# w_out's sums, the start of the feed-forward and the pooling of a hybrid encoder block: other places in the order of work

## The chip, the cores and the metric

The kernel runs on one core of a Trainium2 chip. The metric is the device time of one execution in microseconds (us). The core's engines are named as in the profile: PE (TensorE, matmuls), DVE (VectorE), ACT (ScalarE), POOL (GpSimd) and SP (SyncE, whose queue issues all DMAs here). Each engine works through its own queue in order and waits at an instruction until that instruction's inputs, and the room for its output, are there.

## The reference

One layer of a bidirectional encoder trunk on x of 1024 tokens by 1024 channels, float32:

```python
h = rmsnorm(x, norm_mix)
proj = h @ w_in            # q, k, v, r, decay low-rank, pool input u, gates g_a, g_b
o = gla_fwd(q, k, v) + gla_bwd(q, k, v)          # 4 heads
o = per_head_rmsnorm(o) * gla_norm * silu(r)
y_a = o @ w_branch_gla
pooled = window_means(u, (2, 4, 8, 16)) - u       # 4 groups of 128 channels
y_b = (pooled @ w_pool_group, per group) * pool_scale
x = x + (sigmoid(g_a) * y_a + sigmoid(g_b) * y_b) @ w_out
h2 = rmsnorm(x, norm_ffn)
gate, up = split(h2 @ w_ffn_in)                   # 2 x 2816
x = x + (silu(gate) * up) @ w_ffn_out
return rmsnorm(x, norm_final)
```

## The kernel before, in words

**Products.** Every float32 operand is held as a high part (a cast on ACT, `wh`, `dh`, `gh`, `oh`) and a low part (source minus high part on DVE or POOL, `wl`, `dl`, `gl`, `ol`). A product of two operands is three matmuls, high by high, high by low, low by high (`products`, `mm3`). The large matrix products are done by Strassen's scheme in Winograd's form: seven products P1 to P7 of sums of blocks instead of eight of blocks. S1 to S4 are the sums of the left operand's blocks: S1 = a21 + a22, S2 = S1 - a11, S3 = a11 - a21, S4 = a12 - S2. P6 takes S2, P5 takes S1, P7 takes S3 and P3 takes S4.

**The order.** The whole order of instructions is written out by hand: each engine gets its instructions in the order in which the Python code issues them. What runs beside the matmuls is issued by `pump`, which every `mm3` calls with the length of its product (1 for 512 columns). `soon(delay, step)` issues a step after so many products, `settle` issues at once all that was put off, `begin(generator, delay)` starts a side job that yields the number of products to its next step.

**Gate units (`Gates`, ten of them, n = 0 to 9).** Each runs P1 to P7 of four `mm3` each, in the order `run_of` gives. Units 0 and 1 make the pool input u, which is stored to `u_rows`; 2 to 9 make the gates. Weight parts are made four products ahead (`gates_ahead`, AHEAD). POOL also makes the sums of w_out's blocks (`output_jobs`, L599) beside units 0 to 2. `pooling` is a side job: for each of four groups it loads u, then `pooled` makes for each half the window sums on DVE (L995, L1001, L1007, L1009), a cast on ACT (L1013) and a low part on DVE (L1015). Its yields are multiplied by POOLING = 1.75.

**Branch and w_out (`project`).** Both are seven products of two halves each, so 28 pieces: 0 to 13 for the branch, order `BRANCH`, 14 to 27 for w_out, order `MERGED` = P1, P4, P6, P7, P5, P2, P3. In each piece PE does eight `mm3`: four row tiles m, two k. Each piece has three steps in `line`: its load, its `sums` (of blocks), its `make` (cast and low part of the data, cast and low part of the weights). At piece n `project` makes piece n+2, and asks for the sums by `line_sums`:

```python
line_load()
line_make()
line_sums()
```

`line_make` also calls `line_sums` where the sums of the piece it makes were not begun. Since two pieces are made at the end of the gate units, `line_sums()` at piece n begins those of piece n+3. After the second half of a product `collect` adds each row tile's bank onto x (L1507, DVE) or merges the branch (L1351, L1353, L1354). P1, P6 and P7 of w_out accumulate in one set of four banks, one after the other. In w_out `merged` holds the blocks in slots of their own, 39 slots in all; the sums of P6 write S1 and S2 over blocks, S3 goes to a slot of its own (`s3s`), and S4 is written over block (0, 1) as the sums of P3.

**Norm before the feed-forward.** As P5, P2 and P3 of w_out finish rows of x, `collect_out` takes the squares on ACT, and `normed` scales one row tile after the other: `two_scale` adds both halves' means (L1489, DVE) and takes the power -0.5 (L1490, POOL), and `scale_by` scales the tile (L306, DVE). `features(0)` and `features(1)` then transpose it on PE and make the sums, high and low parts that the feed-forward reads (`split_b`).

**Feed-forward.** 22 units, `run` of `Gated`; the first run of units mixes units 0, 1 and 2, and `features(1)` is made beside it. Units 0 and 1 read ready weight parts from DRAM (`ReadyUnit`). The output stage follows, and the final norm, where `two_scale` is used too.

Of the kernel before, what the change touches and what calls it, by code (L numbers as in the profile page):

```python
# [33 lines left out]
FT = D_FF // P  # L34
# [17 lines left out]
def kernel(  # L52
# [937 lines left out]
    def pooled(g, u, hi, lo):  # L990
        width = WINDOWS[g]
        n = HALF + 2 * PAD
        for half in range(2):
            s = t2(n, s="ws")
            nc.vector.tensor_tensor(s[:, 1:n], u[half][:, : n - 1], u[half][:, 1:n], op=ALU.add)  # L995
            yield 1
            lo_p, hi_p, step = 1, n, 1
            while 2 * step < width:
                a = t2(n, s="ws")
                lo_p, hi_p = lo_p + step, hi_p - step  # L1000
                nc.vector.tensor_tensor(  # L1001
                    a[:, lo_p:hi_p], s[:, lo_p - step : hi_p - step], s[:, lo_p + step : hi_p + step], op=ALU.add
                )
# [5 lines left out]
            nc.vector.scalar_tensor_tensor(  # L1009
                s[:, body], s[:, body], 1.0 / width, u[half][:, body], op0=ALU.mult, op1=ALU.subtract  # L1010
            )
            yield 1
            nc.scalar.copy(hi[:, half, :], s[:, body])  # L1013
            yield 1
            nc.vector.tensor_tensor(lo[:, half, :], s[:, body], as_f32(hi[:, half, :]), op=ALU.subtract)  # L1015
            yield 0.2

# [5 lines left out]
        if len(loads) < len(line):  # L1023
            loads.append(line[len(loads)][0]())

    def line_sums():
        if len(begun_sums) < len(line):
            begun_sums.append(line[len(begun_sums)][1]())

    def line_make():  # L1030
# [76 lines left out]
    MERGED = (1, 4, 6, 7, 5, 2, 3)  # L1107
    WEIGHT_B = {1: (0, 0), 2: (1, 0), 3: (1, 1)}
    merged = {}
    s3s = []  # L1110

    def merged_piece(p, c):
        def load():
            if p in WEIGHT_B:
                i, j = WEIGHT_B[p]
                return weight_load(chunk(w_out, i, j, c))
            return weight_load(t_wo[p][:, 2 * c : 2 * c + 2, :])

        def sums():
            def block(i, j):  # L1120
                return merged[i, j][c][:, :, :]

            if p == 6:
                s3s.append(slot(s="s3"))
                sub(s3s[c][:, :, :], block(0, 0), block(1, 0))
                padd(block(1, 0), block(1, 0), block(1, 1))
                sub(block(0, 0), block(1, 0), block(0, 0))
            elif p == 3:
                sub(block(0, 1), block(0, 1), block(0, 0))

        def make(raw):
            a = s3s[c] if p == 7 else merged[{1: (0, 0), 6: (0, 0), 5: (1, 0), 4: (1, 1), 2: (0, 1), 3: (0, 1)}[p]][c]
            return data_split(a), weight_split(raw)

        return load, sums, make
# [117 lines left out]
    for n, run in enumerate(gate_runs):  # L1253
# [10 lines left out]
        for at, (of, p) in enumerate(run):  # L1264
            if not gates_ahead.step() and at in (5, 7):
                line_make()
            zs[of].run(p)
            for _ in range(2 * (at == 0 and not last)):
                gunits[n + 1].load()
            if p in (7, 4):  # L1270
                zs[of].store(int(p == 4))
            if at == 4:
                flush()
                if n == 2:
                    begin(pooling(), 4)
# [22 lines left out]
    def project(base, products, collect, before, amid=None, first=FIRST, up=UP, pools_of=lambda p: U_BANKS if p == 1 else X_BANKS):  # L1298
        banks = {}
        for at, p in enumerate(products):  # L1300
# [4 lines left out]
            for c in range(2):  # L1305
# [4 lines left out]
                    settle()  # L1310
                line_load()
                line_make()
                line_sums()
                if c == 1 and amid:
                    amid(p)
                a, b = made[n]
# [70 lines left out]
    class ReadyUnit(Unit):  # L1387
# [14 lines left out]

    units = [ReadyUnit(n) if n < READY else Unit(w_ffn_in, (f * P, D_FF + f * P)) for n, f in enumerate(f_order)]

    unit_runs = [[(n, p) for p in (1, 2) for n in range(3)] + [(n, p) for p in (5, 6, 3, 7) for n in range(2)]]
    unit_runs.append([(2, 5), (0, 4), (1, 4), (2, 6), (2, 3), (2, 7)])
    unit_runs += [run_of(n, 2) for n in range(3, FT)]
    unit_runs[-1] = last_run(FT - 1)
    units_ahead = Ahead(units, chain(
        unit_runs[0], [(2, 5), (0, 4), (1, 4), (2, 6), (2, 3), (2, 4), (2, 7)], *(steps_of(n, n == FT - 1) for n in range(3, FT))  # L1410
    ))


# [7 lines left out]
    def low_block(p, i, src, eng=nc.vector):  # L1421
        hi, lo = split_b[p][i]
        eng.tensor_tensor(lo[:, :, :], src, as_f32(hi[:, :, :]), op=ALU.subtract)  # L1423
        if i == 1:
            split_done.add(p)

    def features(half):

# [6 lines left out]
        for k in range(KT):  # L1435
# [13 lines left out]
            elif k % 2:  # L1449

                t = block(0, 0, i)
                if k < 4:
                    sub(t, block(0, 1, i), t)
                    cast_block(5, i, t)
                else:
                    low_block(5, i, t)
                    sub(t, block(1, 1, i), t)
                    cast_block(6, i, t)
            yield 2 if half == 0 else 2.5 if k % 2 else 1
        if half == 0:  # L1460
            return

        for i in range(2):
            cast_block(3, i, block(1, 1, i))
            low_block(6, i, block(0, 0, i))
            yield 3
        for p, b in ((7, block(0, 1, 0)), (7, block(0, 1, 1)), (4, block(1, 0, 0)), (4, block(1, 0, 1))):
            i = len(split_b.get(p, ()))
            if p == 7:
# [16 lines left out]

    def two_scale(ms):
        rs = vec(1, "n3rs")
        nc.vector.tensor_scalar(rs[:, :], ms[:, 0:1], ms[:, 1:2], EPS, op0=ALU.add, op1=ALU.add)  # L1489
        nc.gpsimd.tensor_tensor(rs[:, :], rs[:, :], half_neg[:, :1], op=ALU.pow)  # L1490
        return rs

# [4 lines left out]
    def normed(keep=0):  # L1497
        while len(unnormed) > keep:
            t = unnormed.pop(0)
            scale_by(xn[t], x2[t][:, :], two_scale(mss[t]))  # L1500
            flush()
            later(x2_out[t], x2[t][:, :])

# [26 lines left out]
                units_ahead.step()  # L1530

    def amid_out(p):
        if p == 3:
            for _ in range(2):
                units_ahead.step()

# [121 lines left out]
            both.append((hi, lo))  # L1658
        ready_pieces.append(both)

    begin(features(1), 12)
    zs = {n: Gated(units[n], True) for n in range(3)}
    out_sums, summing = [OutSums(0)], None

    early = {1: "l", 2: "l", 3: "s", 4: "l", 5: "s", 6: "ls"}
    done = {}
    for n, run in enumerate(unit_runs, 1):
        if n == 2:
            finish_side()
            zs[2].two_sums()  # L1670
# [160 lines left out]
```

## Time and profile before

| | us |
|---|---|
| median of three runs | 1402.03 (1400.65 to 1402.65) |
| the profiled execution | 1400.65 |
| its span, first to last instruction | 1398.9 |
| PE busy | 1368.4 (98%) |
| DVE, POOL, ACT busy | 849.5, 748.3, 625.6 |
| granted TensorE clock | 0.999 |

A row of a group names line, engine, operation, output<-inputs and shapes, then the count, the busy time and the mean of one. A row of the timeline begins with start and length in us from the span's start; brackets at its end hold the idle time of the engine before it and what ended it. A row of the waits says who waited for whom, the total in us, how many times, and the longest. In the profile PE is called busy while matmuls overlap, so that idle time of PE is found by the waits and by the start of one matmul after the other.

### The profile page before, as it was taken

What the parts mean: (1) busy time and instruction counts of PE and PEld (TensorE: products, weight loads), DVE (VectorE), ACT (ScalarE), POOL (GpSimd) and SP (SyncE); (2) the same over time, 40 slices, a digit from 0 to 9 for tenths busy, and PEclk for the clock granted to TensorE, in tenths of its full rate; (3) what the DMA queues carried; (4) which work ended last, traced back from release to release, by engine and by line L of the source; (5) the groups of instructions that cost most, each with busy time, mean ns of one, the idle gap of its engine ahead of it and who ended that gap; (6) DMA issues with size and microseconds to landing.
All of it is one profiled execution on the core that took longest, in us unless ns stands there. A gap on an engine that the chain in (4) does not pass through costs nothing.

```text
span 1398.9 us, 18565 instructions
## 1 busy us (share of the span) xinstructions
PE 1368.4 (98%) x6677; PEld 1152.5 (82%) x6677; DVE 849.5 (61%) x1073; ACT 625.6 (45%) x1117; POOL 748.3 (53%) x558
## 2 busy tenths in 40 slices
PE   7999999999999999999999999999999999999997
PEld 6889898978888878788887788888888888888876
DVE  6256757567745975687875865556565556343363
ACT  6364655564233444455346633333333334453253
POOL 3242626031378456568665176666666667454354
PEclk9999999999999999999999999999999999999999
DMA  6212404341268667996515455554444447975461
GB/s 193 76 45 61 136 37 137 102 125 53 76 199 281 213 209 232 354 404 244 200 71 180 166 181 174 173 173 159 145 141 149 140 154 254 388 255 218 165 234 67
DMA packets 167612, 243.62 MB, mean 174 GB/s; under 512 B 10936, under 2 KB 98016, under 8 KB 167520
## 3 DMA queue, kind: packets, MB, share of 16 engines
q1 hardware_dynamic: 167520, 242.45, 51.3%
q8 instruction: 52, 0.85, 0.2%
q14 instruction: 40, 0.33, 0.1%
HBM read 164.55 MB, written 77.86 MB: 173 GB/s over the span
## 4 chain that ended last, share of the span: by engine, by line
PE 81%; DVE 7%; ACT 3%; issue 3%; POOL 3%; DMA 2%; SPq 0%; POOLq 0%; DVEq 0%; ACTq 0%
PE ps L270 74%; PE op L797 2%; POOL wl L197 1%; PE kv L270 1%; PE sc L733 1%; PE op L270 1%; PE tr L317 1%; DMA u_out<-uph 1%; DVE z L666 1%; PE ps L448 1%; DVE fs L866 0%; DMA gor<-g_out 0%; DMA wor<-t_out 0%; DVE so L725 0%; ACT wh L196 0%
## 5 line engine op out<-in xcount | busy, mean ns | idle before, releaser
L197 POOL TENSOR_TENSOR wl<-fs,wh 128x512 fp32r<-128x512 f32 x120 | 166.1, 1388 | 164.8 <-ACT wh L196 139.5
L270 PE MATMUL ps<-gl,wh 128*128 128x512 f32 x616 | 239.8, 389 | 0.9 <-DVE gl L1423 0.9
L270 PE MATMUL ps<-gh,wh 128*128 128x512 f32 x616 | 240.4, 390 | 0.0
L270 PE MATMUL ps<-gh,wl 128*128 128x512 f32 x616 | 239.7, 389 | 0.0
L197 POOL TENSOR_TENSOR wl<-fraw,wh 128x512 fp32r<-128x512 f32 x90 | 129.2, 1436 | 58.2 <-ACT wh L196 57.8
L197 POOL TENSOR_TENSOR ol<-gor,oh 128x1024 fp32r<-128x1024 f32 (+1 forms) x42 | 100.3, 2394 | 93.1 <-ACT oh L196 84.7
L270 PE MATMUL ps<-hh,wh 128*128 128x512 f32 x376 | 149.8, 398 | 0.0
L270 PE MATMUL ps<-hh,wl 128*128 128x512 f32 x376 | 146.7, 390 | 0.0
L270 PE MATMUL ps<-hl,wh 128*128 128x512 f32 x376 | 146.5, 390 | 0.0
L197 POOL TENSOR_TENSOR wl<-raw,wh 128x512 fp32r<-128x512 f32 x47 | 66.3, 1423 | 147.6 <-ACT wh L196 139.2
L270 PEld LDWEIGHTS ps<-gl,wh 128*128 128x128 f32 x616 | 115.7, 188 | 24.9 <-DVE gl L1423 1.3
L270 PEld LDWEIGHTS ps<-gh,wl 128*128 128x128 f32 x616 | 115.7, 188 | 24.2
L270 PEld LDWEIGHTS ps<-gh,wh 128*128 128x128 f32 x616 | 115.7, 188 | 23.6
L270 PE MATMUL ps<-oh,oh 128*128 128x512 f32 x308 | 119.9, 389 | 1.2 <-DVE x L1753 1.2
L270 PE MATMUL ps<-ol,oh 128*128 128x512 f32 x308 | 120.0, 389 | 0.2 <-DVE ol L197 0.2
L270 PE MATMUL ps<-oh,ol 128*128 128x512 f32 x308 | 119.8, 389 | 0.0
L197 POOL TENSOR_TENSOR wl<-wraw,wh 128x512 fp32r<-128x512 f32 x56 | 89.9, 1633 | 45.0 <-ACT wh L196 44.9
L197 DVE TENSOR_TENSOR ol<-wor,oh 128x1024 fp32r<-128x1024 f32 (+1 forms) x42 | 62.0, 1496 | 54.4 <-ACT oh L196 47.1
L196 ACT CAST wh<-fs 128x512 fp32r<-128x512 f32 x120 | 73.8, 615 | 28.8 <-DVE fs L866 28.7
L270 PEld LDWEIGHTS ps<-hh,wl 128*128 128x128 f32 x376 | 70.6, 188 | 15.0
L270 PEld LDWEIGHTS ps<-hl,wh 128*128 128x128 f32 x376 | 70.7, 188 | 13.4
L270 PEld LDWEIGHTS ps<-hh,wh 128*128 128x128 f32 x376 | 70.7, 188 | 13.3
(249 smaller groups left out, 3183.1 us busy)
## 6 DMA issues: line engine op xcount, KB each, us to landing
fraw<-in_w_ffn_in_dram SPq DMA_DIRECT2D x44, 512.0 KB, 5.8
gor<-g_out SPq DMA_DIRECT2D x35, 512.0 KB, 6.7
raw<-in_w_in_dram SPq DMA_DIRECT2D x48, 256.0 KB, 3.0
g_out<-s SPq DMA_DIRECT2D x44, 256.0 KB, 2.3
fraw<-in_w_in_dram SPq DMA_DIRECT2D x20, 512.0 KB, 6.7
wor<-t_out SPq DMA_DIRECT2D x20, 512.0 KB
g_out<-g SPq DMA_DIRECT2D x33, 256.0 KB, 2.6
x<-in_x_dram SPq DMA_DIRECT2D x16, 512.0 KB, 5.1
```

What stands on the lines that cost most here:

```text
L196: nc.scalar.copy(hi, src)
L197: eng.tensor_tensor(lo, src, as_f32(hi), op=ALU.subtract)
L270: nc.tensor.matmul(ps, a[i], b[j], start=first and n == 0, stop=last and n == 2, skip_group_check=onto)
L317: nc.tensor.transpose(ps[:, c], xt[:, k * P : (k + 1) * P], ident[:, :])
L448: nc.tensor.matmul(ps[:, :], lw[k // 4][:, k % 4, :, :].rearrange("p a r -> p (a r)"), hT(k, half)[i], start=k == 0 and i == 0, stop=k == ...
L666: nc.vector.tensor_tensor_scan(cs[:, :], cy, la[:, :], 0.0, op0=ALU.mult, op1=ALU.add)
L733: nc.tensor.matmul(sc[d][:, i * CH : (i + 1) * CH], chunk_of(ke, n, d), chunk_of(qe, n, d), start=True, stop=True,)
L797: nc.tensor.matmul(op[:, :DV], a, b, start=False, stop=j == len(terms) - 1)
```

## The change

- Pooling begins in gate unit 1 instead of 2; in `pooled` the yield between the last sum and the cast is 2 instead of 1, and that between cast and low part 1.5 instead of 1.
- `line_sums` takes the number of the piece up to which sums are begun. `project` calls it with n + 2; after P1 of w_out it is called with piece 18, the first half of P6.
- S4 gets slots of its own and is made as the sums of P7; P3 reads it there.
- `two_scale`'s add is on POOL, and `normed` puts `scale_by` off by 1.5 products.
- The feed-forward's first run is P1, P2, P5 of units 0 to 2 and then P6, P3, P7 of units 0 and 1; the second run begins with P4 of both. `features(1)` begins after 11 products instead of 12, and its casts and low parts are put off by 1.5 and 3.3 products (`split_soon`).

```diff
@@ pooled
-            yield 1
+            yield 2
             nc.scalar.copy(hi[:, half, :], s[:, body])
-            yield 1
+            yield 1.5
@@
-    def line_sums():
-        if len(begun_sums) < len(line):
+    def line_sums(to=None):
+        to = len(begun_sums) if to is None else to
+        while len(begun_sums) < min(len(line), to + 1):
             begun_sums.append(line[len(begun_sums)][1]())
@@ merged_piece
-            elif p == 3:
-                sub(block(0, 1), block(0, 1), block(0, 0))
+            elif p == 7:
+                s4s.append(slot(s="s4"))
+                sub(s4s[c][:, :, :], block(0, 1), block(0, 0))
...
+            a = s3s[c] if p == 7 else s4s[c] if p == 3 else merged[
+                {1: (0, 0), 6: (0, 0), 5: (1, 0), 4: (1, 1), 2: (0, 1)}[p]
+            ][c]
@@ gate units
-                if n == 2:
+                if n == 1:
                     begin(pooling(), 4)
@@ project
-                line_sums()
+                line_sums(n + 2)
@@ order of the feed-forward
-    unit_runs = [[(n, p) for p in (1, 2) for n in range(3)] + [(n, p) for p in (5, 6, 3, 7) for n in range(2)]]
-    unit_runs.append([(2, 5), (0, 4), (1, 4), (2, 6), (2, 3), (2, 7)])
+    unit_runs = [[(n, p) for p in (1, 2, 5) for n in range(3)] + [(n, p) for p in (6, 3, 7) for n in range(2)]]
+    unit_runs.append([(0, 4), (1, 4), (2, 6), (2, 3), (2, 7)])
...
+    def split_soon(p, i, src):
+        soon(1.5, partial(cast_block, p, i, src))
+        soon(3.3, partial(low_block, p, i, src))
@@ features(1)
                 if k < 4:
                     sub(t, block(0, 1, i), t)
-                    cast_block(5, i, t)
+                    split_soon(5, i, t)
                 else:
-                    low_block(5, i, t)
+                    settle()
                     sub(t, block(1, 1, i), t)
-                    cast_block(6, i, t)
+                    split_soon(6, i, t)
...
             cast_block(3, i, block(1, 1, i))
-            low_block(6, i, block(0, 0, i))
             yield 3
+            settle()
@@ two_scale, normed
-        nc.vector.tensor_scalar(rs[:, :], ms[:, 0:1], ms[:, 1:2], EPS, op0=ALU.add, op1=ALU.add)
+        nc.gpsimd.tensor_scalar(rs[:, :], ms[:, 0:1], ms[:, 1:2], EPS, op0=ALU.add, op1=ALU.add)
...
-            scale_by(xn[t], x2[t][:, :], two_scale(mss[t]))
+            soon(1.5, partial(scale_by, xn[t], x2[t][:, :], two_scale(mss[t])))
@@ amid_out
-        if p == 3:
+        if p == 1:
+            line_sums(len(BRANCH) * 2 + 4)
+        elif p == 3:
@@ start of the feed-forward
-    begin(features(1), 12)
+    begin(features(1), 11)
     zs = {n: Gated(units[n], True) for n in range(3)}
+    zs[2].two_sums()
...
-            while n == 1 and p > 2 and p not in split_done:
-                next(side[0][0])
+                if put_off:
+                    settle()
+                else:
+                    next(side[0][0])
...
-            if n > 1 and 0 < at + (n == 2) < 6:
+            if n > 1 and 0 < at + 2 * (n == 2) < 6:
                 next(summing, None)
```

More of the change, by code (lines that the diff above doesn't have):

```diff
@@ L1109 @@
     merged = {}
-    s3s = []
+    s3s, s4s = [], []
     def merged_piece(p, c):
@@ L1127, in sums @@
                 sub(block(0, 0), block(1, 0), block(0, 0))
-            elif p == 3:
-                sub(block(0, 1), block(0, 1), block(0, 0))
+            elif p == 7:
+                s4s.append(slot(s="s4"))
+                sub(s4s[c][:, :, :], block(0, 1), block(0, 0))
         def make(raw):
-            a = s3s[c] if p == 7 else merged[{1: (0, 0), 6: (0, 0), 5: (1, 0), 4: (1, 1), 2: (0, 1), 3: (0, 1)}[p]][c]
+            a = s3s[c] if p == 7 else s4s[c] if p == 3 else merged[
+                {1: (0, 0), 6: (0, 0), 5: (1, 0), 4: (1, 1), 2: (0, 1)}[p]
+            ][c]
             return data_split(a), weight_split(raw)
@@ L1409 @@
     units_ahead = Ahead(units, chain(
-        unit_runs[0], [(2, 5), (0, 4), (1, 4), (2, 6), (2, 3), (2, 4), (2, 7)], *(steps_of(n, n == FT - 1) for n in range(3, FT))
+        unit_runs[0], [(0, 4), (1, 4), (2, 6), (2, 3), (2, 4), (2, 7)], *(steps_of(n, n == FT - 1) for n in range(3, FT))
     ))
@@ L1669 @@
             finish_side()
-            zs[2].two_sums()
         elif n > 2:
```

## The prediction

> **What bounds the kernel now.** I read the page's first part, then the waits of PE, then the stretches by engine.
>
> ```profile
> span 1398.9 us, 18565 instructions
> PE 1368.4 (98%) x6677; PEld 1152.5 (82%) x6677; DVE 849.5 (61%) x1073; ACT 625.6 (45%) x1117; POOL 748.3 (53%) x558
> ```
>
> PE is the bound, and the change adds and removes no matmul. So only time in which PE stands can move. The waits of PE between 500 and 790 us:
>
> ```profile
> PE tr L1438 <- DVE xn L306: 1.6, 1, 1.6
> PE ps L270 <- ACT ga L1212: 1.4, 1, 1.4
> PE ps L270 <- DVE x L1507: 1.2, 1, 1.2
> PE yb L270 <- DMA pl<-p_out: 0.9, 1, 0.9
> PE ps L270 <- DVE gl L1423: 0.9, 1, 0.9
> PE ps L270 <- DVE dl L162: 0.7, 1, 0.7
> ```
>
> These six single waits lie where the change works. The rhythm of PE in a stretch without waits, from the chain in order of time:
>
> ```profile
> 367.55 5.48 PE ps L270 x24
> 373.03 0.44 PE tp L970 x4
> ```
>
> A matmul of 512 columns takes 5.48 / 24 = 0.228 us from start to start, so a product (three matmuls) takes 0.68, a piece of `project` (eight products) 5.46, a product of a unit (four) 2.73. A single matmul lasts 0.39 (row below), so a wait costs its idle time and the lost overlap, 0.39 - 0.228 = 0.16. Without the DMA wait, five waits make 5.8 + 5 x 0.16 = **6.6 us**: the most that the change can give. The DMA wait (p_out loads of the last gate units, 56 us after pooling's last sum) stays: these are loads of pooled rows that lie stored long before, and no edit touches what SP holds ahead of them.
>
> **Pooling, 1.6 us.** The stretches, and ACT where PE waited for it:
>
> ```profile
> 424.00:446.00 22.00, 22.00 (x99) 18.23 (x98) 8.32 (x9) 8.55 (x15) 19.16 (x15) 1.00 0.88 286
> 446.00:507.00 61.00, 61.00 (x271) 50.53 (x270) 55.15 (x62) 26.83 (x49) 33.03 (x32) 1.00 0.69 221
> 511.23 0.62 ACT L1013 CAST ph<-ws 128x512 fp32r<-128x512 f32 x1 [2.50 <-DVE ws L1009]
> 511.76 0.58 ACT L1212 COPY ga<-ps 128x512 f32<-128x512 f32 x1
> ```
>
> The columns of the first two are stretch, length, PE, PEld, DVE, ACT, POOL, clock, DMA share, GB/s. While pooling runs, DVE is busy 55.15 of 61. It falls behind, ACT's cast L1013 waits for it, and the copy L1212, which frees a bank, is queued behind the cast. The new yields hold the cast back 3.5 products instead of 1.75 (2.4 us for 1.2) and the low part 2.6 for 1.75. The same DVE work of a half of the last group is spread over 13.5 products instead of 10.85. The cast waited 2.50; a hold longer by 1.2 and 1.8 us more in which DVE can catch up cover that. I count the whole wait as gone, 1.4 + 0.16.
>
> One unit sooner, the first group meets POOL's subtractions (POOL busy 19.16 of 22). Six DVE sums there slow POOL: a 512-wide sum beside DVE takes up to the double of the 1.3 us that it takes alone (rows of w_out below for both engines), so 0 to 8 us in sum, some 3 if half of each overlaps. The weight parts behind it are made four products of a unit (10.9 us) ahead; that hides it. SP is moved past too: the loads of u follow the stores of the same rows directly and hold the queue for a store's landing. The unit's weight loads behind them have the same 10.9 us. Cost nothing; without that cover up to 3 us.
>
> **w_out: sums one piece later, S4 at P7.** In the kernel before, piece n begins the sums of piece n+3, one piece (5.46 us) before that data is cast. In the changed one `line_sums(n + 2)` finds nothing to do, because `line_make` has just forced these sums; only piece 18 (P6, first half) keeps its place, by `amid_out`. So the sums of pieces 12, 13 and 19 come one piece later, straight ahead of the cast of the same data.
>
> ```profile
> 654.00:673.00 19.00, 19.00 (x86) 15.73 (x85) 18.69 (x20) 8.57 (x12) 16.02 (x11) 1.00 0.68 250
> 642.73 2.32 DVE L1084 TENSOR_TENSOR ob<-ob,t 128x1024 f32<-128x1024 f32 x1
> 654.00 2.31 DVE L1084 TENSOR_TENSOR ob<-ob,t 128x1024 f32<-128x1024 f32 x1
> 656.40 1.05 ACT L1056 CAST dh<-ob 128x1024 fp32r<-128x1024 f32 x1 [5.05 <-DVE ob L1084]
> 656.24 4.55 DVE L162 TENSOR_TENSOR dl<-ob,dh 128x1024 fp32r<-128x1024 f32 x2
> 668.97 2.85 DVE L162 TENSOR_TENSOR dl<-mg,dh 128x1024 fp32r<-128x1024 f32 x2
> 672.91 0.39 PE L270 MATMUL ps<-wh,dl 128*128 128x512 f32 x1
> ```
>
> DVE is busy 18.69 of these 19 us: whatever is put in comes out as delay. L1084 of piece 12, now at 642.73, moves to 654.0, behind the merges of P7; its low part must wait for the cast (1.05); then the same for piece 13. Step by step: sum 12 to 656.3, cast to 657.4, low part to 658.7 (1.3, half beside POOL), sum 13 to 660.9, cast to 662.0, low part to 663.7. Today the merges of P3 begin after the two low parts, at 656.24 + 4.55 = 660.8; now 2.9 later. They take 668.97 - 660.8 = 8.2, to 671.9, and the low part of piece 14 is there at 673.7. PE's first matmul that reads it is the row at 672.91. New wait 0.8, with the overlap **0.9** (0 to 1.5).
>
> ```profile
> 678.26 2.32 DVE L1125 TENSOR_TENSOR s<-mg,mg 128x1024 f32<-128x1024 f32 x1
> 684.10 1.22 DVE L1127 TENSOR_TENSOR mg<-mg,mg 128x1024 f32<-128x1024 f32 x1 [3.53 <-POOL mg L1126]
> 688.77 1.85 DVE L1125 TENSOR_TENSOR s<-mg,mg 128x1024 f32<-128x1024 f32 x1
> 693.13 1.23 DVE L1127 TENSOR_TENSOR mg<-mg,mg 128x1024 f32<-128x1024 f32 x1 [2.51 <-POOL mg L1126]
> 694.28 2.42 DVE L162 TENSOR_TENSOR dl<-mg,dh 128x1024 fp32r<-128x1024 f32 x2
> 696.62 2.48 DVE L1507 TENSOR_TENSOR x<-ps,x 128x512 f32<-128x512 f32 x4
> 699.01 3.45 DVE L162 TENSOR_TENSOR dl<-s,dh 128x1024 fp32r<-128x1024 f32 x2
> 702.38 0.68 DVE L1507 TENSOR_TENSOR x<-ps,x 128x512 f32<-128x512 f32 x1
> 696.04 10.09 POOL L197 TENSOR_TENSOR wl<-wraw,wh 128x512 fp32r<-128x512 f32 x6 [2.94 <-ACT wh L196]
> ```
>
> The wait for dl (0.7 + 0.16) goes: the low part of piece 18 no longer stands behind the sums of piece 19. DVE comes to the sums of 18 some 4 us late (the 2.9, and 1.1 because the low part of 15 now meets POOL), wins 2 back where it stood 3.53 for POOL, and reaches L1127 of 18 at 686.2 and, with the low part of 18 (1.4) ahead, of 19 at 696.1 (today 693.13). It ends at 697.3, the cast at 698.4, the low part, beside POOL, at 700.2; the weights' casts wait behind that cast, and POOL's second split of them ends at 702.1. PE is at piece 19 at 672.46 + 5 x 5.46 + 0.9 = 700.7 (672.46 is two matmuls ahead of the row at 672.91) and wants that split four matmuls later, at 701.6: **0.5** (0 to 1.2).
>
> The adds of P4 (2.48) end at 702.5. Behind them now stand four steps where there were two: S4 of the first half, a low part, S4 of the second half, a low part. Of the pair at 699.01 one took 1.2 and one 2.3, beside six POOL splits that took 10.09; now POOL's six run beside all four. At 2.1 each DVE comes to the add of P6 at 711.0, and its first bank is free at 711.7; today this add runs at 702.38. P7 accumulates in that bank: PE gets to piece 20 at 672.46 + 6 x 5.46 = 705.2, and 1.4 later for the waits above, 706.6. Wait 5.1 less the overlap already in hand, **4.9**. From below: no lateness and 1.2 for each sum, 704 to 705, no wait; from above 6.0. I take 4.9 because the row nearest to it, the pair at 699.01, is in this very stretch.
>
> **P2 to P3, 1.4 us, and norms.**
>
> ```profile
> 736.18 2.31 DVE L1129 TENSOR_TENSOR mg<-mg,mg 128x1024 f32<-128x1024 f32 x1
> 738.40 2.42 DVE L162 TENSOR_TENSOR dl<-mg,dh 128x1024 fp32r<-128x1024 f32 x2
> 740.74 2.48 DVE L1507 TENSOR_TENSOR x<-ps,x 128x512 f32<-128x512 f32 x4
> 757.57 0.75 DVE L306 TENSOR_SCALAR xn<-x,n3rs 128x1024 f32<-128x1024 f32 x1 [3.20 <-POOL n3rs L1490]
> 778.11 1.22 DVE L1423 TENSOR_TENSOR gl<-hb,gh 128x1024 fp32r<-128x1024 f32 x1
> ```
>
> Without L1129 here the adds come 2.3 sooner, more than the wait of 1.2 + 0.16: gone. The sum of squares' add moves to POOL and L306 is put off, so DVE no longer stands 3.20 for POOL with three adds behind. The last xn comes about 3 us sooner; the transposes want it 1.6 + 0.16 sooner and begin a product (0.68) sooner, 2.4 together: the wait goes. POOL now waits for ACT's squares; behind it are weight parts of unit 2, due four products later.
>
> **Feed-forward, 1.1 us.** With P5 of a third unit behind P2, the second low part of P5's data is issued at product 19 instead of 23.5, 3.1 us sooner: the wait of 0.9 + 0.16 goes. P6's data is due four products later than before. Unit 2's P5 comes six products sooner with a DVE sum (0.7), a cast and a POOL split (1.3 alone); made four products ahead they are hidden, else they cost their own time. The stores of the first output sums go out one unit later, and are read only in the output stage: nothing. S4's slots replace blocks that are free sooner: nothing.
>
> **The end.**
>
> ```profile
> L1489 DVE TENSOR_SCALAR n3rs<-n3ms x8: 201/212/215, 1333.1 to 1393.7; 128x1 f32<-128x1 f32 x8
> L1490 POOL TENSOR_TENSOR n3rs<-n3rs,half_neg x16: 548/549/987, 726.8 to 1394.0; 128x1 f32<-128x1 f32 x16
> L690 POOL TENSOR_TENSOR fac<-fac x16: 192/204/1139, 87.6 to 301.1; 128x4 f32<-128x4 f32 x16
> ```
>
> The last of these eight is on the path that ends the kernel. On POOL it costs 0.20 by L690, up to 0.55 by L1490, against 0.21 and a hop: -0.1 to +0.35, I take 0.1. [...]
>
> **Sum.** Gone 6.6; new 0.9 + 0.5 + 4.9 = 6.3; end 0.1: -0.2 us. The profiled execution took 1400.65 (span 1398.9 and 1.75 around it) and would take 1400.45. The median of the runs is 1402.03, 1.4 above it, so 1401.8.
>
> **Rivals.** *Clean gain* (0.32): the sums fall into gaps, new waits stay at their lower ends, 1.3 in all: 1402.0 - 6.6 + 1.3 = 1396.7. For it: today the add at 702.38 ends 3 us before P7 needs it. Against it: the 18.69 of 19.
>
> *PE loses its clock at P7* (0.27, slower): if DVE's backlog is at the upper ends, 1.5 + 1.2 + 6.0 = 8.7, PE stands long enough to be throttled.
>
> ```profile
> 7.41 3.46 PE L317 MATMUL tr<-ident,xn 128*128 128x128 f32 x16 [0.23 <-DVE xn L306]
> core 0: 1398.9 us, clock 0.999
> ```
>
> At the start, after 7 us without work, 16 transposes took 0.216 each, later 0.11 (0.44 for 4): 1.7 us lost. In sum 8.7 + 1.7 + 0.1 - 6.6 = +3.9: 1405.9. It decides the sign once new losses pass 9.4. No wait of the six, the longest 1.6, can have lowered it for long: the mean granted clock of the span is 0.999. [...]
>
> *Pooling's holds do nothing* (0.07): 1.6 stays, 1403.4.
>
> **Chances.** My forecast 0.34. A change under 0.2% (2.8 us) is about what a measurement of this kernel can't tell from none. Forecast and last rival fall within it: 0.41; faster 0.32; slower 0.27. The forecast's own range is 1399.3 to 1404.7; the range takes in the two outer cases: 1396.6 to 1405.9.
>
> **What would show it.** In the changed profile: a wait of the first matmul of P7 for the add L1507, near 706 us, 3 to 6 us long, would prove the main step; a wait for dl near 673; no wait for L1212 near 507, none for xn and gl after 757. If P7 starts without a wait the forecast is wrong by up to 5 us; if granted clock drops after it, the second rival holds.

## The result and the profile after

The changed kernel takes 1404.58 us (median of 15 runs, 1403.26 to 1406.58), the kernel before 1402.03 us (15 runs beside it). The ratio is 1.0023, with a 95% interval from 1.0016 to 1.003: slower by some 3 us, a little over 0.2%. The forecast was 1401.8 us and "no change". The profiled execution of the changed kernel took 1403.89 us, and its span is 3.3 us longer than that of before (1398.9). The first lines of its page:

```profile
span 1402.2 us, 18583 instructions
PE 1370.0 (98%) x6677; PEld 1153.4 (82%) x6677; DVE 849.2 (61%) x1057; ACT 626.1 (45%) x1117; POOL 758.7 (54%) x574
```

PE has the same 6677 matmuls and is 1.6 us longer busy with them (1368.4 before). VectorE has 16 instructions fewer and POOL 16 more. These are the sixteen adds of the norms. The rest of the 3.3 us must be waits. The waits of PE from 440 us to the end, with the total, the number and the longest in us:

```profile
PE ps L270 <- DVE x L1515: 3.7, 1, 3.7
PE ps L270 <- DVE ol L197: 2.4, 1, 2.4
PE ps L270 <- DVE x L1766: 1.3, 1, 1.3
PE yb L270 <- DMA ph<-p_out: 0.7, 1, 0.7
PE yb L270 <- DMA pl<-p_out: 0.7, 1, 0.7
PE tr L1446 <- DVE xn L306: 0.5, 1, 0.5
PE ps L270 <- POOL wl L197: 0.5, 2, 0.3
PE ps L270 <- ACT ga L1216: 0.3, 1, 0.3
```

The lines of the file have moved: L1515 is the add that was L1507, L1766 was L1753, L1216 was L1212, L1446 was L1438, L1131 is the new S4, L1497 and L1498 are the two steps of `two_scale` and L1737 is the scaling of the final norm. Of the six waits that the prediction listed, those for ga at 512 us, for x between P2 and P3, for dl and for gl are gone, and that for xn has shrunk from 1.6 to 0.5 us. Two large ones are new: 3.7 us for x (P7's first matmul, at 709 us) and 2.4 us for ol (before: 0.2), in the output stage at 1350 us.

Both kernels issue the same number of matmuls of the same sizes, so each can be set against the one of the same number in the other. The table gives by how much its start moves at each place; the sum is the longer span. A row reads the first matmuls at its place; those right behind still move by up to 0.2 us, which stands in the next row. Where the shift has settled, the new wait for ga is 0.56 us (the matmuls had gained 0.19 before it), the old one 1.72, dl 1.01, POOL's wl 1.05 and the slow stretch 1.7.

| place, us in after | what PE meets there | predicted | measured |
|---|---|---|---|
| 462, 511 | pooling: a new wait for ga; the old one gone | -1.56 | +0.34, -1.57 |
| 567 | loads of p_out | 0 | +0.36 |
| 671 | low part of piece 14 | +0.9 | 0 |
| 694 | dl | -0.86 | -0.86 |
| 700 | POOL's wl of piece 19 | +0.5 | +0.79 |
| 709 | P7's first bank | +4.9 | +3.95 |
| 710 to 713.5 | matmuls at half clock | only in a rival | +1.52 |
| 745 | bank of P3 | -1.36 | -1.37 |
| 767 | xn | -1.76 | -1.35 |
| 780 | gl | -1.06 | -0.80 |
| 1350 | final norm: ol | +0.1 for the whole end | +2.00 |
| after 1350 | tail | | +0.23 |
| sum | | -0.2 (working of the prediction) | +3.24 |

**P7's wait** is read on VectorE's timeline (start, duration, instruction, idle time before it in brackets):

```profile
698.09 2.47 DVE L1515 TENSOR_TENSOR x<-ps,x 128x512 f32<-128x512 f32 x4
700.48 1.21 DVE L1131 TENSOR_TENSOR s<-mg,mg 128x1024 f32<-128x1024 f32 x1
701.62 2.31 DVE L162 TENSOR_TENSOR dl<-s,dh 128x1024 fp32r<-128x1024 f32 x1
703.86 2.31 DVE L1131 TENSOR_TENSOR s<-mg,mg 128x1024 f32<-128x1024 f32 x1
706.08 2.29 DVE L162 TENSOR_TENSOR dl<-s,dh 128x1024 fp32r<-128x1024 f32 x1
708.29 2.47 DVE L1515 TENSOR_TENSOR x<-ps,x 128x512 f32<-128x512 f32 x4
```

Between the adds of P4 at 698.09 and those of P6 at 708.29 stand the four steps that the prediction counted. VectorE is never idle here. All four run beside POOL's splits of 128x512 (1.29 us each at 699.29 and 709.47, beside the adds). The first step begins at 700.48 and takes 1.21; POOL's split of 700.54 ends at 702.85, after 2.31. From there on each engine takes 2.25 to 2.31 for a step. So VectorE's step takes 1.21 where it starts ahead of POOL's split, and 2.29 to 2.31 where it starts behind one. The add of P6 starts 5.9 us later than in before (702.38), and P7's first matmul stands 3.7 us for it.

**The clock behind the wait.** The stretches of after (stretch, length, then busy time and count of PE, PEld, DVE, ACT, POOL, granted clock, DMA share, GB/s):

```profile
705.40:709.10 3.70, 0.06 (x1) 0.01 (x1) 3.70 (x4) 1.65 (x3) 3.70 (x2) 1.00 0.04 14
709.10:713.60 4.50, 4.48 (x13) 3.56 (x14) 4.50 (x5) 0.00 (x0) 3.93 (x3) 0.62 0.01 4
713.60:720.00 6.40, 6.40 (x30) 5.31 (x29) 2.63 (x5) 2.19 (x3) 2.55 (x2) 1.00 0.00 0
```

In the 4.5 us behind the wait the clock is 0.62 on average: PE does 13 matmuls where 20 fit. From 710 to 713.5 us they follow each other at 0.43 us instead of 0.228.

**The final norm.** POOL and then VectorE in after:

```profile
1336.60 0.30 POOL L1497 TENSOR_SCALAR n3rs<-n3ms 128x1 f32<-128x1 f32 x1
1336.99 0.56 POOL L1498 TENSOR_TENSOR n3rs<-n3rs,half_neg 128x1 f32<-128x1 f32 x1
1341.40 0.86 POOL L1497 TENSOR_SCALAR n3rs<-n3ms 128x1 f32<-128x1 f32 x1
1342.34 0.84 POOL L1498 TENSOR_TENSOR n3rs<-n3rs,half_neg 128x1 f32<-128x1 f32 x1
1343.15 5.18 POOL L197 TENSOR_TENSOR ol<-gor,oh 128x1024 fp32r<-128x1024 f32 x2
```

```profile
1341.34 1.42 DVE L1737 SCALAR_TENSOR_TENSOR res<-x,n3rs,gfin 128x512 f32<-128x512 f32 x2 [0.46 <-POOL n3rs L1498]
1343.22 5.66 DVE L1737 SCALAR_TENSOR_TENSOR res<-x,n3rs,gfin 128x512 f32<-128x512 f32 x2 [0.46 <-POOL n3rs L1498]
1348.80 2.35 DVE L197 TENSOR_TENSOR ol<-wor,oh 128x1024 fp32r<-128x1024 f32 x2
```

The same place in the kernel before, POOL and then VectorE:

```profile
1339.03 0.99 POOL L1490 TENSOR_TENSOR n3rs<-n3rs,half_neg 128x1 f32<-128x1 f32 x1 [0.46 <-DVE n3rs L1489]
1339.98 5.34 POOL L197 TENSOR_TENSOR ol<-gor,oh 128x1024 fp32r<-128x1024 f32 x2
```

```profile
1338.86 7.01 DVE L1724 SCALAR_TENSOR_TENSOR res<-x,n3rs,gfin 128x512 f32<-128x512 f32 x4
1345.80 2.35 DVE L197 TENSOR_TENSOR ol<-wor,oh 128x1024 fp32r<-128x1024 f32 x2
```

In before VectorE made each add in 0.2 us between its other work and POOL raised to the power. Now POOL does both for four tiles in turn. A pair costs 0.30 + 0.56 alone and 0.86 + 0.84 beside VectorE, and VectorE stands 0.46 us for each tile. POOL comes to its two low parts at 1343.15 instead of 1339.98. VectorE's last two scalings run beside those low parts in both kernels (5.66 here, the last two of the four in the 7.01 before). Here they wait for POOL's fourth power, which ends at 1343.18, so VectorE's own low part ol starts 3.0 us later than before. PE is 1.0 us later by then, so it loses 2.0.

### The profile page after: what moved, and what is told of

Same layout as the page of the kernel before. It is cut to its first block, busy times and chain, and to the rows that moved or that the text cites. A ratio compares the mean times of both kernels' runs of the same rounds, so it can differ in the third digit from the quotient of the medians.

```text
span 1402.2 us, 18583 instructions
## 1 busy us (share of the span) xinstructions
PE 1370.0 (98%) x6677; PEld 1153.4 (82%) x6677; DVE 849.2 (61%) x1057; ACT 626.1 (45%) x1117; POOL 758.7 (54%) x574
## 4 chain that ended last, share of the span: by engine, by line
PE 79%; DVE 6%; POOL 4%; ACT 3%; DMA 3%; issue 3%; SPq 0%; POOLq 0%; DVEq 0%; ACTq 0%
PE ps L270 72%; PE op L797 2%; POOL wl L197 1%; PE kv L270 1%; DMA u_out<-uph 1%; PE sc L733 1%; PE op L270 1%; DVE fs L866 1%; POOL gl L1427 1%; PE tr L317 1%; DMA u<-u_rows 1%; DVE z L666 1%; PE ps L448 1%; ACT wh L196 0%; DMA gor<-g_out 0%
```

## The experiments

Theory: three places pay, namely the two S4 sums ahead of P6's add, the clock behind the wait that they make, and the final norm's add on POOL; the waits that the change was to remove are removed. Rivals: the wait comes from the way the sums are called and not from S4's place; the final norm is off the path. Where no ratio is given the time is that of a single execution, which the start of the kernel alone can move by some 1.5 us (last section); there the waits decide.

**x1_final_dve: the final norm's add back on VectorE.**

```
-            soon(1.5, partial(scale_by, ..., two_scale(mss[t])))
+            soon(1.5, partial(scale_by, ..., two_scale(mss[t], nc.gpsimd)))
     def two_scale(ms, eng=nc.vector):
         ...
-        nc.gpsimd.tensor_scalar(rs[:, :], ...)
+        eng.tensor_scalar(rs[:, :], ...)
```

> After with the add of two_scale put back on VectorE for the four tiles of the final norm only; the norm ahead of the feed-forward keeps it on GpSimd. Theory (three places pay: P7's first bank, the clock behind it, the final norm): in the trace of after TensorE waits 2.4 us for a low part of the final norm (ol), 0.2 us in before, and the same matmul stands 1.99 us later than in before, with 0.16 us more at the tail. The wait goes back to 0.2 to 0.5 us and the time falls by 2.0 to 2.2 us, to 1402.4. Rival (the add is off the path that ends last, the tail's wait comes from the work that arrives late from P7): the wait for ol stays above 1.5 us and the time stays at 1404.6, within 0.5 us.

Measured: ratio to before 1.0008 (0.9999 to 1.0017), where the changed kernel has 1.0023. The difference, 0.0015 x 1402 = 2.1 us, is the expected one, though the two intervals just meet. The trace is plainer. Its waits:

```profile
PE ps L270 <- DVE x L1515: 3.7, 1, 3.7
PE ps L270 <- DVE ol L197: 0.5, 1, 0.5
```

The wait for ol is down from 2.4 to 0.5 us, that of P7 is untouched. The final norm is a cause of its own.

**x2_s4_at_p5: S4 with the sums of P5.**

```
-            elif p == 7:
+            elif p == 5:
                 s4s.append(slot(s="s4"))
```

> After with the two S4 sums of w_out's weights made with the sums of P5 and not with those of P7, still in their own slots; everything else as in after. Theory (the two S4 sums and the splits between them stand on VectorE ahead of the add of P6 that frees P7's first bank): the 3.7 us wait at P7's first matmul falls under 0.5 us, the nine matmul steps of 0.43 us behind it go back to 0.228 us, and the time falls by 3.95 + 1.52 us, to 1399.1. Rival (it is the earlier calling of the sums for all pieces, not S4's place): a wait of 2 to 3 us stays at P7's first matmul and the time falls by at most 2 us, to 1402.5.

(S4 is a sum of blocks of the branch's output, the left operand, not of w_out's weights as the expectation has it.) Measured: 1399.39 us, ratio 0.9991 (0.9982 to 0.9999), 4.5 us under the changed kernel (0.0032 x 1402). P7's wait and the slow steps behind it are gone. VectorE there:

```profile
699.02 2.48 DVE L1515 TENSOR_TENSOR x<-ps,x 128x512 f32<-128x512 f32 x4
701.41 3.46 DVE L162 TENSOR_TENSOR dl<-s,dh 128x1024 fp32r<-128x1024 f32 x2
704.79 2.47 DVE L1515 TENSOR_TENSOR x<-ps,x 128x512 f32<-128x512 f32 x4
```

Two steps of 3.46 us instead of four of 8.1, and the sums called just as in the changed kernel: the rival falls. The four steps now stand ahead of P7's adds, from 707.19 to 715.04 us, and no matmul waits for them there. At the matmuls the gain is the whole 3.95 + 1.52 us. That the ratios differ by only 4.5 us can have its cause at another place, which is shown for the profiled execution alone: the wait for ol (2.4 us, as in after) has here a stretch at half clock behind it, which it hadn't in after.

```profile
1345.47:1349.50 4.03, 4.03 (x11) 3.16 (x12) 1.44 (x2) 0.62 (x1) 0.00 (x0) 0.58 1.00 307
```

A clock of 0.58 over 4.03 us is a loss of 1.7 us.

**x5_both: both edits together.** Both diffs above.

> Both edits together: S4 made with the sums of P5, and the final norm's add on VectorE. Theory: the two savings add up, 5.5 + 2.1 us, so 1397.0, some 5 us under the kernel before. Rival (what is saved at P7 is given back by a later wait, or the two savings are the same time): 1399 or more.

Measured: 1397.12 us, ratio 0.997 (0.9959 to 0.9981), some 4 us faster than before and 7.4 us faster than the changed kernel. The two savings add up. In its profile no wait of over 1.4 us is left after 440 us, and no matmul is slowed behind one.

**x4_early_sums: the sums called one at a time.**

```
-                line_sums(n + 2)
+                line_sums()
```

> After with the weight sums of w_out called one at a time as in the kernel before (no calling ahead to piece n + 2), S4 still made as the sums of P7 in own slots. Theory (the count of VectorE operations ahead of P6's add decides): the two S4 sums and their splits still come between P6's first add and its second, so a wait of 2 to 3.5 us stays at P7's first matmul, and the wait for dl at about 695 us comes back with 0.9 us. Time 1402.5 to 1405. Rival (the earlier calling makes the wait): P7's wait falls under 0.5 us and the time is about 1400.

Measured: 1399.97 us in one run. The edit did something else than its expectation says. The call in the middle of P1 stayed, so that calling one at a time runs one piece ahead of the changed kernel, and the first S4 falls ahead of P4's adds. Three steps (5.8 us) stand between the adds of P4 and P6, not four. Its waits:

```profile
PE ps L270 <- DVE x L1515: 1.3, 1, 1.3
PE ps L270 <- DVE dl L162: 0.7, 1, 0.7
```

The wait was 1.3 us (with the lost overlap 1.5, as later expectations count it), under the 2 to 3.5 that the theory gave for four steps and over the rival's 0.5. No slow matmul follows it. Read as a smaller dose it fits the theory: one step less on VectorE, 2.3 us, and 2.4 us less wait.

**b_s4: before, with S4 alone moved to P7 in own slots.**

```
-            elif p == 3:
-                sub(block(0, 1), block(0, 1), block(0, 0))
+            elif p == 7:
+                s4s.append(slot(s="s4"))
+                sub(s4s[c][:, :, :], block(0, 1), block(0, 0))
```

> Before with only S4 in own slots, made as the sums of P7; the weight sums are called one at a time as in before, and pooling, norm and feed-forward are as before. Theory (what counts is how many 1024-wide sums and splits VectorE has between P4's adds and P6's adds: four in the changed kernel with 3.7 us of wait, three in x4_early_sums with 1.5 us): here they are one sum and two splits, so a wait of 1.2 to 1.7 us at P7's first matmul, no slow steps there; the wait for dl at 695 us stays, the 1.4 us wait between P2 and P3 at 741 us goes; time as before, within 0.5 us, apart from the clock at the start. Rival (S4's place alone makes the long wait): 3 us or more at P7's first matmul.

Measured: 1403.2 us, before 1402.5 beside it. The wait at P7 is 1.3 us and the dl wait stays, as expected. The wait between P2 and P3 does not go: 1.1 us after 1.2. VectorE there:

```profile
737.50 1.82 DVE L306 TENSOR_SCALAR xn<-x,n3rs 128x1024 f32<-128x1024 f32 x1 [0.66 <-POOL n3rs L1493]
739.24 4.55 DVE L162 TENSOR_TENSOR dl<-s,dh 128x1024 fp32r<-128x1024 f32 x2
743.71 2.47 DVE L1510 TENSOR_TENSOR x<-ps,x 128x512 f32<-128x512 f32 x4
```

The sum of 2.31 us is gone, but the two low parts behind it now take 4.55 us. In before they took 2.42, and the sum, from 736.18 on, stood beside POOL's splits (734.42 to 737.40) in their place. By these times (an estimate) taking work off a shared stretch moved the collision to the next instruction.

**b_sums: before, with the calling of the sums alone.** `line_sums(n + 2)` and the call in the middle of P1, as in the diff of the change; S4 in place at P3. The expectation calls these sums earlier; as the prediction worked out, for most pieces they come a piece later, right ahead of the cast of the same data.

> Before with only the earlier weight sums of w_out (line_sums to piece n + 2, and the call in the middle of P1); S4 is still made in place as the sums of P3, and pooling, norm and feed-forward are as before. Theory (the two S4 sums ahead of P6's add make the 3.7 us wait, not the earlier calling): no wait over 0.5 us at P7's first matmul and no steps of 0.43 us behind it; the wait for dl at 695 us (1.1 us in before) is gone, and two steps for POOL's wl at 700 us come, +0.8 us together; the 1.4 us wait between P2 and P3 at 741 us stays. Time as before, within 0.5 us. Rival (the earlier calling pays at P7 as well): a wait of 1.5 us or more at P7's first matmul, time 1.5 us or more above before.

Measured: 1403.71 us, before 1402.3. At P7 the theory holds: no wait, dl gone, two steps at 700 us. But the wait between P2 and P3 does not stay at 1.2, it grows to 3.7 us, and a slow stretch follows. VectorE ahead of those adds:

```profile
735.76 1.22 DVE L1130 TENSOR_TENSOR mg<-mg,mg 128x1024 f32<-128x1024 f32 x1
738.09 1.23 DVE L162 TENSOR_TENSOR dl<-mg,dh 128x1024 fp32r<-128x1024 f32 x1 [1.11 <-ACT dh L1057]
739.23 2.31 DVE L1130 TENSOR_TENSOR mg<-mg,mg 128x1024 f32<-128x1024 f32 x1
742.66 1.23 DVE L162 TENSOR_TENSOR dl<-mg,dh 128x1024 fp32r<-128x1024 f32 x1 [1.11 <-ACT dh L1057]
743.80 2.48 DVE L1508 TENSOR_TENSOR x<-ps,x 128x512 f32<-128x512 f32 x4
```

These are the same four steps as at P7 in the changed kernel, and each low part stands 1.11 us for ACT's cast besides, since its sum comes right ahead of it. So the later calling and S4's place belong together: with sum and split of both halves side by side, S4 costs 3.7 us ahead of either of these two adds. Ahead of P7's adds, where x2_s4_at_p5 puts the same four steps, it costs nothing: that is due to the place, not to the number.

**b_norm: before, with the norm edit alone.** `two_scale`'s add on POOL and the scaling put off, as in the diff of the change.

> Before with only the norm edit: two_scale's add on GpSimd, and the scaling ahead of the feed-forward put off by 1.5. Theory (one edit with a gain of about 1.35 us at the feed-forward's start and a price of about 2.0 us in the final norm): TensorE's wait for xn at 765 us falls from 1.6 to about 0.5 us, its wait for ol at 1348 us grows from 0.2 to about 2.4 us, the time is 0.6 to 0.9 us above before. Rival (the gain at 765 us comes from S4's removal out of VectorE's way, not from the norm edit): the wait for xn stays at 1.6 us and the time is 2.0 us above before.

Measured: 1404.91 us, before 1402.3. The waits that matter:

```profile
PE ps L270 <- DVE ol L197: 2.4, 1, 2.4
PE tr L1438 <- DVE xn L306: 1.1, 1, 1.1
PE ps L270 <- DVE x L1507: 0.7, 1, 0.7
```

The price is there in full (2.2 us at the matmul, and 1.5 of slow matmuls behind it). The gain is smaller at xn than expected, 0.5 us, and there is 0.7 us at the bank between P2 and P3, which the prediction had given to S4's move. With b_s4: neither edit removes that wait alone; the changed kernel, with both, has lost it.

**b_pool and b_ff: before, with pooling alone, and with the feed-forward alone.** The hunks of the change for `yield 2`, `yield 1.5` and `n == 1`; and those for `unit_runs`, `split_soon`, `features` and `begin(features(1), 11)`.

> Before with only the pooling edit: it begins one unit sooner, and its two holds are longer. Theory: the pooling wait at 512 us (1.6 us) is gone, 0.3 us comes at 462 us for ga, up to 0.4 us comes at 566 to 568 us where TensorE waits for p_out; time 0.9 to 1.2 us under before. Rival (pooling gives it back at p_out, whose load is due at a fixed time): the two steps at 566 to 568 us grow by 1.5 us and the time is as before.

> Before with only the feed-forward edit: the first run takes P1, P2, P5 of three units, the second unit's sums and the splits are spread with soon and settle. Theory: the wait for gl at 779 us (1.1 us) is gone, everything else as before, time 1.1 us under before. Rival (the third unit's P5 ahead of P6 makes a new wait for a weight or for a data split): a wait of 0.5 us or more appears between 780 and 830 us and the time is as before.

Measured: pooling 1398.8 us, with 1.57 us gained at 512 us, 0.27 lost at 462 us and nothing lost at p_out, which refutes its rival. (The profiled execution of before that the traces are compared with took 1400.65, so the profiled gain is 1.85; 0.5 of it comes at the very end and not from pooling.) Feed-forward 1400.52 us: the wait for gl goes, 1.1 us, and no new wait comes between 780 and 830 us, but xn waits longer:

```profile
PE tr L1442 <- DVE xn L306: 2.2, 1, 2.2
```

The transpose that waits is released at the same time, 765.2 us, as in before, but it now has fewer matmuls ahead of it. Of the 1.1 us some 0.5 remain at 780 us. Neither the theory nor its rival had that.

**x6_dose_long and x8_dose_mid: more work ahead of P6's add.** In x6_dose_long the second S4 is made twice, in x8_dose_mid (on x4_early_sums) half of it:

```
-                sub(s4s[c][:, :, :], block(0, 1), block(0, 0))
+                for _ in range(1 + c):
+                    sub(s4s[c][:, :, :], block(0, 1), block(0, 0))
```

> After with the second S4 sum made twice over (one more VectorE operation of 1024 columns ahead of P6's add; the same values). It makes the wait at P7's first matmul longer and leaves all else. Theory (a TensorE wait of this length costs one stretch at half clock, whose size does not grow with the wait): the wait grows from 3.7 to about 6.0 us, behind it stand again 8 to 10 steps of 0.43 us in some 3.4 us, a loss of 1.4 to 1.8 us; time 2.3 us above after. Rival (the loss grows with the wait): more than 12 slow steps, a loss of 2.3 us or more.

> The kernel of x4_early_sums, in which TensorE waits 1.5 us at P7's first matmul without a slow stretch behind it, with half of the second S4 sum made twice over (one more VectorE operation of 512 columns). The wait grows by 0.7 to 1.2 us to 2.2 to 2.7 us. Theory (waits of 3.7 us cost the stretch each time, three of three; of the four waits of 2.4 us two did): at this length either can come; if a stretch comes it is one of 8 to 10 steps and not a part of one. Rival (the loss is in proportion to the wait): 2 to 6 slow steps.

Measured: waits of 5.9 us and 3.0 us at P7's first matmul, 1407.74 and 1404.41 us. The stretches, first of x6_dose_long behind its wait, then of x8_dose_mid at its wait (706.64 to 709.66 us) and at its later wait for ol (1346.68 to 1349.10):

```profile
712.00:718.00 6.00, 5.96 (x14) 4.71 (x15) 3.96 (x5) 0.00 (x0) 1.67 (x2) 0.51 0.01 3
```

```profile
704.56:707.97 3.41, 2.08 (x10) 1.38 (x8) 3.41 (x2) 1.86 (x3) 3.41 (x3) 1.00 0.00 0
707.97:711.39 3.42, 1.73 (x8) 1.46 (x9) 3.42 (x6) 0.33 (x1) 3.33 (x2) 1.00 0.02 5
711.39:714.80 3.41, 3.41 (x17) 2.81 (x16) 2.19 (x2) 0.02 (x1) 0.00 (x0) 1.00 0.00 0
1346.27:1349.68 3.41, 0.99 (x5) 0.49 (x4) 3.41 (x3) 0.00 (x0) 1.09 (x1) 1.00 0.27 111
1349.68:1353.09 3.41, 3.41 (x10) 2.64 (x9) 0.83 (x2) 0.62 (x1) 0.00 (x0) 0.50 0.96 291
```

After 5.9 us the loss is 6.00 x 0.49 = 2.9 us, more than the 1.4 to 1.8 expected. It is not in proportion to the wait either: in x1_final_dve a wait of 3.7 us cost 2.8 us, in the changed kernel the same wait 1.7. After 3.0 us there was no loss at all, and after 2.4 us in the same execution there was one, 3.41 x 0.50 = 1.7 us. So whether a wait of this length costs the clock, and whether it costs some 1.7 or 2.8 us, is not set by its length alone.

The granted clock in the traces shows what else goes with it. Past 300 us every stretch at half clock ahead of the last outputs lasts 3.41 us, or twice that (x1_final_dve, x6_dose_long). Within one execution the clock changes a whole number of times 3.4133 us apart: in the changed kernel half clock begins at 710.06 and again at 1399.56 us, 202 x 3.4133 later, in x8_dose_mid at 18.48 and 1349.68, 390 x 3.4133. So each trace can be cut into windows of 3.41 us at whose borders alone its clock changes; where they lie differs from one execution to the next (a border at 706.65 us in the changed kernel, at 707.97 in x8_dose_mid). The rows of x8_dose_mid are cut along them. Its wait of 3.0 us is shared by two windows, in which PE is still busy for 2.08 and 1.73 us, and the clock stays. Its wait of 2.4 us falls into one; PE is busy for 0.99 us, and the next window has half clock. From 300 to 1385 us the fourteen traces have eight windows at full clock in which PE was busy for 1.56 us or less (it stood for 1.85 or more), and each is followed by one at half clock; after all the others, 1.70 us and more, the clock stays. In the changed kernel the two lowest of them are 0.94 us from 706.65 to 710.06, with half clock behind it, and 1.70 us from 1348.35 to 1351.77, without. Where PE stood on into the slow window (1.22 us in x1_final_dve, 1.02 in x6_dose_long) a second slow one followed; that is the loss of 2.8 and 2.9 us. This is read from the traces; no run set where the windows lie.

The steps between the adds of P4 and P6 and the wait that they made, over these runs:

| steps of 1024 columns on VectorE | kernel | wait at P7, us |
|---|---|---|
| 2 | before, x2_s4_at_p5 | 0 |
| 3 | x4_early_sums, b_s4 | 1.3 |
| 3 and a half one | x8_dose_mid | 3.0 |
| 4 | after, x1_final_dve | 3.7 |
| 5 | x6_dose_long | 5.9 |

**x7_dve_add: x5_both with the add on VectorE ahead of the feed-forward too.**

```
-        nc.gpsimd.tensor_scalar(rs[:, :], ms[:, 0:1], ...)
+        nc.vector.tensor_scalar(rs[:, :], ms[:, 0:1], ...)
```

> x5_both with two_scale's add on VectorE in the norm ahead of the feed-forward as well, so that of the norm edit only the putting off by 1.5 is left. Theory (the gain at the feed-forward's start comes from the scaling put off, the engine of the 128x1 add does little): TensorE's wait for xn at about 761 us stays within 0.3 us of 0.5 us and the time within 0.5 us of x5_both's. Rival (the add on GpSimd takes VectorE's queue out of the chain): the wait for xn grows by 0.6 to 1.2 us, and the time by as much.

Measured: 1399.46 us, ratio 0.9979 (0.9969 to 0.9988) where x5_both has 0.997: some 1.3 us more (0.0009 x 1402), though the two intervals overlap. The trace is plainer:

```profile
PE tr L1446 <- DVE xn L306: 1.9, 1, 1.9
```

Against 0.5 us in x5_both. The rival holds, by a little more than the 0.6 to 1.2 us it gave: the gain at the feed-forward's start comes from the add's move to POOL, not from putting the scaling off. The same move that costs 2 us in the final norm earns 1.4 us here.

## Why the prediction was wrong

It named the right places and missed the sign of the whole. The removed waits came nearly as worked out: 5.95 us of 6.6, by the table. P7's wait, the main step, was put at 4.9 and measured 3.95, with four steps of 8.1 us where the prediction took 8.4; this step holds, by the trace and by x2_s4_at_p5. Piece 19 cost 0.79 for 0.5. The predicted 0.9 us for the low part of piece 14 did not come: that low part is done at 671.6 us, two earlier than the 673.7 worked out. The step that failed there is the sum of VectorE's delay in the full stretch before 673 us: the low parts behind the merges of P3 start 1.5 us later than in before (670.43 for 668.97), not 2.9. Pooling added 0.34 us of a new wait and the loads of p_out 0.36 more, which the prediction held at nothing.

Two steps decide the sign.

**"The end."** The prediction costed only the last of the eight adds in the final norm, at -0.1 to +0.35, as if each add stood alone at the tail. Four of them come in a row at 1336 us, on POOL, which then has two low parts to make for the matmuls of 1350 us. What had to be counted is POOL's queue: 3.2 us later for its own low parts and, since VectorE's last scalings wait for POOL's fourth power, 3.0 us later for VectorE's. Measured +2.0 us, and x1_final_dve gives 2.1 back. The prediction's lower end for the cost on POOL, 0.20 us, came from a row of another shape (L690, 128x4). These 128x1 adds take 0.30 us on POOL against 0.20 on VectorE, both alone, and 0.86 beside VectorE.

**The clock.** The rival had the place and the price (1.7 us; measured 1.52 at the matmuls), and its own sign for it, a lower granted clock behind P7's wait, came. Its condition failed: it asked for a wait at the upper end, 6.0, and new losses past 9.4 us. A wait of 3.7 us was enough here each of three times, so the forecast's own 4.9 us should have been priced with it. In the forecast the price should have been a term of the sum: with it and with 2.2 instead of 0.1 at the end, -0.2 + 1.5 + 2.1 = +3.4, against the measured 3.24. That this comes so near is luck in part: P7's wait and piece 14 were put 1.85 us too dear, and the terms other than these, the end and the clock 1.64 too cheap.

The reason given for the wait between P2 and P3 ("without L1129 here the adds come 2.3 sooner") was wrong though its size was right: b_s4 took L1129 out and the wait stayed. It took the norm edit as well. And the gain at xn was put down to VectorE's not standing for POOL; x7_dve_add bears that out.

What stays open: why the matmuls wait longer for the loads of p_out in the changed kernel while b_pool shows next to nothing of it. It varies from execution to execution: in the eight traces that have the changed kernel's code up to there, the matmuls lose between nothing (x6_dose_long) and 0.8 us (x5_both) at that place. Where the clock's windows fall is given by nothing in the kernel that these runs show.

## What to carry to other kernels

Before a sum is moved, count the steps that the receiving stretch has between two instructions that free a bank, and price each at its time beside the other engine: here, ahead of P6's add, two of them were free, three cost 1.3 us and four cost 3.7, while four ahead of P7's add were free. When a helper's instruction changes engine, look up every place that calls it, since the same edit won 1.4 us at one call and lost 2.0 us at another. A wait of TensorE should be given a second price, that of the matmuls behind it at half clock: here none up to 1.6 us, 1.5 to 2.9 us in all four executions with a wait of 3.7 us or more at a bank, and in between a chance, by how the wait fell on the windows of 3.41 us.

## What the runs showed of the hardware

**Half clock behind short waits.** After waits of TensorE of 1.0 to 1.6 us (past 300 us) no run shows slow matmuls. After 1.9 us (x7_dve_add) there were some, after 2.2 us (b_ff) none; after 2.4 us in three executions of six; after 3.0 us none; after 3.7 us in three of three; after 5.9 us again. The losses were 1.5 to 1.7 us, or 2.8 to 2.9 in two cases. All of this follows the largest part of the wait that falls into one window of 3.41 us: 1.85 us (x7_dve_add) and more was paid for, 1.71 us (the changed kernel at 1348 us, of a wait of 2.4) and less was not. By that (an estimate) a wait of 3.7 us, twice 1.85, can't lie so that it escapes. Waits of 1.9 and 2.4 us are shorter than one window and were paid for: a window in which PE stood for a little over half, 1.85 of 3.41 us, was enough.

**The start.** In eight of the fourteen profiled executions, with the same instructions, the matmuls between 11 and 24 us ran partly at half clock, for one window, and lost 1.3 to 1.6 us. The same stretch in x5_both and in b_s4:

```profile
11.00:24.00 13.00, 9.94 (x74) 8.85 (x74) 9.08 (x23) 11.81 (x28) 5.99 (x7) 1.00 0.72 230
```

```profile
11.00:24.00 13.00, 10.61 (x64) 9.53 (x63) 8.64 (x22) 10.27 (x24) 5.99 (x7) 0.87 0.70 230
```

A clock of 0.87 over 13 us is 1.7 us. It shows in the times: of the 23 executions of the kernel before beside the first four experiments, the eleven with a mean clock of 0.999 took 1399.95 to 1400.98 us, and eleven of the twelve with 0.998 took 1401.65 to 1402.77. The 1.4 us that the prediction set between the profiled execution of before and the median is about this step. That is a good part of the scatter of this kernel's times, and it is why single executions were read here by their waits and not by their times.
